# A 3x3 convolution with 2x2 max pooling: a new instruction order, casts moved from VectorE to ScalarE, and a wait added on GpSimd

## The chip, the cores and the metric

The kernel runs on one core of a Trainium2 chip. The metric is the device time of one execution in microseconds (us); lower is better. The kernel before takes 102.99 us (median of 3 runs, 102.98 to 103.02).

The core has five instruction streams that run at the same time, each strictly in its own program order: TensorE (PE in the profile: matmuls, with PEld for its weight loads), VectorE (DVE), ScalarE (ACT), GpSimd (POOL) and SyncE (SP, which here only issues DMAs). They meet through semaphores.

## The reference

```python
x_pad = np.pad(x, ((0, 0), (0, 0), (1, 1), (1, 1)))          # x: 16 x 64 x 64 x 64
for kh in range(3):
    for kw in range(3):
        conv[b, co] += weight[co, ci, kh, kw] * x_pad[b, ci, kh:kh+64, kw:kw+64]
output[b, c, i, j] = np.max(conv[b, c, 2*i:2*i+2, 2*j:2*j+2])  # 16 x 128 x 32 x 32
```

The input has 64 channels, the output 128. All is float32; the kernel multiplies in bf16.

## The kernel before, in words

**Tiles.** Two images lie in the 128 partitions (2 x 64 channels), so there are eight image pairs. A pair is cut into four stretches of eight output rows; the 32 stretches are numbered s = 0 to 31 (s // 4 is the pair, except that 2 and 3 stand for the last and the third stretch of pair 0). Each stretch has two halves h = 0, 1, one per image: a matmul uses 64 rows of the array, and two such matmuls, one per half, run beside each other. A step is named with its stretch and half: `P2.7.1` is product P2 of stretch 7, image 1.

**The computation of a stretch.** An even and an odd conv row of a pooled pair share input rows, and max(a, b) is formed from sums and differences of rows. For most stretches ("W" in `TYPES`) three row tensors are made first: a sum (`S.s`, tile ws), a difference (`E.s`, tile we) and the differences of rows two apart (`D.s`, tile wd, twice as large). Each can be made on VectorE (line 88) or on GpSimd (line 89); three tuples of stretch numbers choose. Stretches of type "K" need only a sum on VectorE (`KS.s`, tile ks) and read the rows themselves. The weights are combined to match: `g0`, `g1`, `g2` are the three kernel rows cast to bf16, `D2`, `D0`, `GM`, `GP` their sums and differences; PE transposes each block (`T...`, line 165) and ScalarE or VectorE copies it from PSUM to the tile wt (`V...`, lines 182 to 188).

**The chain of a half stretch.** PE accumulates the first products into a PSUM bank (P2 and P0, or PA1 and PA2). ScalarE copies that bank, after P2, into a second bank (`SE`, line 389) and, after P0, into SBUF with a sign (`EV`, lines 373 and 375), which frees the first bank. PE adds P3 to the second bank; VectorE takes the row maximum of bank and SBUF copy (`MX`, line 399); PE adds P1 (or PR), the product of the row sum. ScalarE copies the odd columns out (`OD`, line 405), VectorE takes the column maximum (`CM`, line 419), which frees the second bank, and SyncE stores the stretch (`ST`). There are eight banks.

**The first image pair** goes another way, in pieces: its rows come as float32 in three tiles, kfirst (two loads), ksecond (two) and middle (three). The K stretches 0 and 2 need bf16 rows, so kfirst and ksecond are cast into the tile kx0: `XOa`, `XOb`, `XEa`, `XEb` (odd and even rows of kfirst, first and second part) and `X1a`, `X1b`, `X2a`, `X2b` for ksecond. Their products are done in half stretches, `F.k.part` for stretch 0, `H.k.part` for stretch 2, six matmuls each. Stretch 1 lies in middle: `Ea`, `Eb`, `Da`, `Db`, `S.1` make its row tensors, `G.k.part` are its products, `SEa`, `SEb` its copies. PR.0 and PR.2 finish stretches 0 and 2.

**The order.** Nothing is scheduled by a compiler: the text `ORDER` lists every step, and each engine runs its steps in that order. Tile adds waits only where data or buffers ask for them, plus one kind that is written by hand: every row operation that the kernel routes through `on_gpsimd` waits for the last operation routed through `on_vector`, so that a GpSimd row operation starts only when VectorE's last one is done.

**Loads.** `LX.p.part` (line 124) loads half an image pair, converting to bf16, from GpSimd's queue; the seven first loads and all stores are issued by SyncE. `L` is the third load of middle; it waits for the cast `XOa`. `LX.1.0` waits for the cast `XOb`.

Of the kernel before, what the change touches and what calls it, by code (L numbers as in the profile page):

```python
# [11 lines left out]
def kernel(  # L12
# [11 lines left out]
    nc = tc.nc  # L24
# [47 lines left out]
    odd_cast = {}  # L72
# [69 lines left out]
    def slots(m):  # L142
        return wq[:, m : m + 3, :]
# [302 lines left out]
            queue.dma_start(out=dst[:, h : h + 1], in_=src[:, h : h + 1])  # L446


    def cast_rows(n, src, to, lo, hi):
        out, in_ = kx0[:, to + lo : to + hi : 2, :], src[:, lo:hi:2, :]  # L450
        if n in CAST_BY_SCALAR:
            odd_cast[n] = nc.scalar.copy(out=out, in_=in_)
        else:
            odd_cast[n] = nc.vector.tensor_copy(out=out, in_=in_)  # L454

    steps = {
        "g0": lambda: nc.scalar.copy(out=slots(G0), in_=g0),
        "g1": lambda: nc.vector.tensor_copy(out=slots(G1), in_=g1),  # L458
        "g2": lambda: nc.scalar.copy(out=slots(G2), in_=g2),
        "D2": lambda: sbuf_sum(True, out=slots(D2), in0=g2, in1=g1, op=SUB),  # L460
        "D0": lambda: sbuf_sum(True, out=slots(D0), in0=g0, in1=g1, op=SUB),
        "GS": lambda: sbuf_sum(False, out=gsum, in0=g0, in1=g2, op=ADD),
# [28 lines left out]
    for m in PRODUCTS:  # L491
        steps[m] = lambda s, h, m=m: product(m, s, h)

    ORDER = """
        D0 g2 g0 TD0 g1 D2 TD2 VD0 XEa uG1 TG1 F.2.0 TG0 XOa L VD2 F.0.0 TG2 GS GP uGP VG1 XOb F.0.1 LX.1.0 VG2
        VG0 F.1.0 F.1.1 XEb F.2.1 EV.0.1 EV.0.0 GM uGM LX.2.0 F.3.1 F.3.0 TMP VMP KS.0 X1a X2a X1b X2b KS.2
        H.0.0 H.1.0 H.0.1 H.1.1 EV.2.1 EV.2.0 Ea LX.1.1 LX.3.0 Da MX.0.0 MX.0.1 H.2.0 PR.0.1 H.3.0 G.0.0 Eb
        G.0.1 H.2.1 H.3.1 PR.0.0 SEa.0 SEa.1 SEb.0 SEb.1 E.3 P2.3.1 G.1.0 S.1 MX.2.0 OD.0.0 CM.0.0 G.2.0 OD.0.1
        CM.0.1 ST.0 LX.3.1 LX.2.1 Db G.1.1 EV.1.1 MX.2.1 G.2.1 MX.1.1 PR.2.0 PA1.4.0 PA2.4.0 EV.1.0 MX.1.0
        PA1.4.1 P1.1.0 PR.2.1 OD.2.0 CM.2.0 SE.3.1 P1.1.1 EV.4.0 S.3 OD.2.1 CM.2.1 ST.2 OD.1.0 CM.1.0 OD.1.1  # L500
        CM.1.1 ST.1 D.3 P0.3.1 PB1.4.0 EV.3.1 P2.3.0 P3.3.1 MX.3.1 PA2.4.1 SE.3.0 PB2.4.0 MX.4.0 EV.4.1 E.5
        P2.5.1 P2.5.0 SE.5.0 P1.3.1 PB1.4.1 P0.3.0 EV.3.0 D.5 P0.5.0 SE.5.1 EV.5.0 E.8 OD.3.1 PB2.4.1 KS.4
        PR.4.0 OD.4.0 P3.5.0 P0.5.1 EV.5.1 D.7 P3.5.1 E.7 P2.7.1 P2.7.0 D.8 D.9 SE.7.0 CM.3.1 CM.4.0 MX.4.1
        PR.4.1 MX.5.0 P3.3.0 MX.3.0 SE.7.1 P0.7.1 MX.5.1 P0.7.0 EV.7.0 P3.7.1 P3.7.0 P1.3.0 MX.7.0 OD.4.1 CM.4.1
        EV.7.1 MX.7.1 S.5 P1.5.1 P1.5.0 OD.5.1 CM.5.1 OD.3.0 CM.3.0 OD.5.0 CM.5.0 ST.5 ST.4 S.7 P1.7.0 E.6
        P2.6.0 P2.6.1 OD.7.0 CM.7.0 D.6 LX.7.1 LX.4.0 LX.6.0 LX.4.1 S.6 D.10 D.11 S.11 E.9 KS.12 PA1.12.1 P1.7.1
        PA1.12.0 PA2.12.1 SE.6.1 P3.6.1 P0.6.1 SE.6.0 OD.7.1 PA2.12.0 EV.12.0 EV.12.1 CM.7.1 P2.8.0 SE.8.0
        P0.6.0 EV.6.0 P3.6.0 P0.8.0 PB1.12.1 PB2.12.1 P2.8.1 P3.8.0 MX.6.0 P1.6.0 EV.6.1 P2.9.1 PB1.12.0 MX.6.1
        P1.6.1 MX.12.1 PR.12.1 EV.8.0 MX.8.0 PB2.12.0 SE.8.1 P0.8.1 OD.6.0 CM.6.0 OD.6.1 CM.6.1 MX.12.0 SE.9.1
        P0.9.1 OD.12.1 CM.12.1 S.8 E.10 P1.8.0 OD.8.0 CM.8.0 S.14 S.10 D.14 P3.8.1 P3.9.1 P2.10.0 EV.8.1 SE.10.0  # L510
        EV.9.1 PR.12.0 OD.12.0 MX.8.1 P1.8.1 P2.9.0 SE.9.0 P0.10.0 EV.10.0 P2.10.1 LX.5.0 MX.9.1 S.9 E.14 E.11
# [81 lines left out]
```

## Time and profile before

| | |
|---|---|
| median of 3 runs | 102.99 us (102.98 to 103.02) |
| the profiled execution | 103.01 us |
| its span, first to last instruction | 101.1 us |
| TensorE clock granted, mean | 0.993 of full |
| PE, DVE, ACT, POOL busy | 93%, 89%, 86%, 69% of the span |
| HBM read, written | 17.20 MB, 8.39 MB |

The profile is one execution. "start us, us" in a timeline row are the start from the span's begin and the length of a run of like instructions (x6: six of them); in brackets stands how long the engine had been idle and what ended that. In a row of groups come busy time, mean length in ns, idle time before. L207 is line 207 of the kernel; in the changed kernel lines from 449 on stand up to six lower.

### The profile page before, as it was taken

The numbers are of one execution on the slowest core, as the hardware profiler recorded it, in microseconds if no ns is written. First come the engines' busy times: TensorE is split into PE (matmuls) and PEld (weight loads), VectorE is DVE, ScalarE is ACT, GpSimd is POOL, SyncE is SP. The second block draws the span as 40 slices with busy tenths as digits, with TensorE's granted clock in tenths as the row PEclk, the third lists the DMA queues.
The fourth block names the chain that finished last, engine by engine and source line by source line (L and its number), as shares of the span: only waits on it lengthen the run. The fifth ranks groups of instructions, "written<-read, shape, count | busy, mean of one in ns | idle before, by whom it ended". The sixth has DMA issues, their size and how long they took to land.

```text
span 101.1 us, 2529 instructions
## 1 busy us (share of the span) xinstructions
PE 94.3 (93%) x903; PEld 58.9 (58%) x903; DVE 89.9 (89%) x190; ACT 86.0 (85%) x194; POOL 70.2 (69%) x79
## 2 busy tenths in 40 slices
PE   6889999999999999999999999999999999999900
PEld 2257878844555656777678677675555546545500
DVE  1589989999999999999999989999898969999950
ACT  5356778999699899999999999898999999999830
POOL 7268999906995985774987693994969699417000
PEclk9999999999999999999999999999999999999997
DMA  2999899999947999999947984835024837423062
GB/s 58 297 342 300 171 199 216 221 232 226 244 78 131 247 228 220 228 221 358 343 31 124 282 180 42 169 114 208 3 76 141 304 111 252 163 104 110 0 227 84
DMA packets 11900, 18.41 MB, mean 182 GB/s; under 512 B 880, under 2 KB 9200, under 8 KB 11888
## 3 DMA queue, kind: packets, MB, share of 16 engines
q0 software_dynamic: 2016, 7.34, 39.9%
q1 hardware_dynamic: 9728, 10.78, 32.0%
q8 instruction: 7, 0.11, 0.4%
q10 hardware_dynamic: 144, 0.13, 0.4%
q14 instruction: 5, 0.04, 0.1%
HBM read 17.20 MB, written 8.39 MB: 253 GB/s over the span
## 4 chain that ended last, share of the span: by engine, by line
PE 87%; DVE 4%; DMA 3%; ACT 1%; issue 1%; DVEq 0%; ACTq 0%
PE acc L207 86%; DMA wraw<-in_weight_dram 3%; DVE acc L399 1%; PE acc L165 1%; DVE wq L88 1%; DVE o L434 1%; DVE kx L454 1%; ACT acc L389 1%; ACT od L427 1%; DVE wq L458 0%; DVE wt L188 0%; DVEq L399 0%; ACTq L389 0%
## 5 line engine op out<-in xcount | busy, mean ns | idle before, releaser
L207 PEld LDWEIGHTS <-wt 64*128 64x128 bf16 x870 | 56.4, 94 | 32.6 <-issue 4.7
L207 PE MATMUL acc<-wd,wt 64*128 64x512 bf16 (+2 forms) x336 | 65.9, 369 | 0.1
L399 DVE TENSOR_TENSOR acc<-acc,ev 128x512 f32<-128x512 f32 x64 | 42.4, 692 | 1.4 <-ACT ev L375 0.5
L207 PE MATMUL acc<-we,wt 64*128 64x512 bf16 (+3 forms) x168 | 39.2, 369 | 0.0
L207 PE MATMUL acc<-ws,wt 64*128 64x512 bf16 (+3 forms) x168 | 37.7, 369 | 0.2 <-DVE acc L399 0.2
L375 ACT ACTIVATE ev<-acc 128x512 f32<-128x512 f32 x54 | 32.2, 607 | 1.4 <-PE acc L207 1.2
L389 ACT COPY acc<-acc 128x512 f32<-128x512 f32 x52 | 30.7, 596 | 0.9 <-DVE o L419 0.2
L419 DVE TENSOR_TENSOR o<-acc,od 128x256 f32<-128x256 f32 x62 | 24.4, 417 | 2.4 <-ACT od L405 1.5
L89 POOL TENSOR_TENSOR ws<-xb 128x512 bf16<-128x512 bf16 x15 | 17.1, 1148 | 11.6 <-DVE wd L88 7.3
L405 ACT COPY od<-acc 128x256 f32<-128x256 f32 x62 | 22.5, 382 | 2.1 <-PE acc L207 1.8
L89 POOL TENSOR_TENSOR we<-xb 128x512 bf16<-128x512 bf16 x16 | 18.4, 1150 | 6.0 <-PE acc L207 2.3
L89 POOL TENSOR_TENSOR wd<-xb 128x1024 bf16<-128x1024 bf16 x9 | 19.1, 2123 | 1.9 <-DVE we L88 1.1
L207 PE MATMUL acc<-xb,wt 64*128 64x504 bf16 (+3 forms) x72 | 15.0, 372 | 0.0
L88 DVE TENSOR_TENSOR wd<-xb 128x1024 bf16<-128x1024 bf16 x16 | 10.7, 682 | 0.0
L124 POOL DMA_DIRECT2D xb<-in_x_dram x14 | 7.9, 574 | 0.1
L207 PE MATMUL acc<-ks,wt 64*128 64x504 bf16 (+1 forms) x30 | 7.2, 377 | 0.0
L373 ACT COPY ev<-acc 128x512 f32<-128x512 f32 x10 | 5.6, 590 | 1.4 <-PE acc L207 1.3
L207 PE MATMUL acc<-kx,wt 64*128 64x252 bf16 (+3 forms) x96 | 6.0, 267 | 0.4 <-DVE kx L454 0.4
L89 POOL TENSOR_TENSOR wd<-middle 128x512 bf16<-128x512 f32 (+1 forms) x3 | 4.9, 1643 | 0.2 <-DVE we L88 0.2
L551 PE MATMUL acc<-const-bfloat16-1.0 128*128 128x512 bf16 x8 | 3.5, 621 | 0.8 <-PEq L574 0.8
L88 DVE TENSOR_TENSOR ws<-xb 128x512 bf16<-128x512 bf16 x10 | 4.1, 418 | 0.0
L88 DVE TENSOR_TENSOR we<-xb 128x512 bf16<-128x512 bf16 x9 | 3.7, 425 | 0.0
(33 smaller groups left out, 29.4 us busy)
## 6 DMA issues: line engine op xcount, KB each, us to landing
out_dram<-o SPq DMA_DIRECT2D x31, 256.0 KB, 2.9
xb<-in_x_dram POOLq DMA_DIRECT2D x7, 528.0 KB, 9.0
xb<-in_x_dram POOLq DMA_DIRECT2D x7, 496.0 KB, 11.0
middle<-in_x_dram SPq DMA_DIRECT2D x1, 512.0 KB, 5.3
ksecond<-in_x_dram SPq DMA_DIRECT2D x1, 320.0 KB, 5.8
middle<-in_x_dram SPq DMA_DIRECT2D x1, 320.0 KB, 6.2
wraw<-in_weight_dram SPq DMA_DIRECT2D x1, 288.0 KB, 2.9
kfirst<-in_x_dram SPq DMA_DIRECT2D x1, 288.0 KB, 3.2
```

The lines of the kernel that those rows point to most:

```text
L88: return on_vector(nc.vector.tensor_tensor(**args))
L89: return on_gpsimd(nc.gpsimd.tensor_tensor(**args))
L124: inst = nc.gpsimd.dma_start(out=xb[p][:, 1 + lo : 1 + hi, :], in_=rows_of(p, lo, hi))
L165: nc.tensor.transpose(tp[:, k * CO : (k + 1) * CO], wq[:, j : j + 2, :].rearrange("a b c -> a (b c)"), ident,)
L207: nc.tensor.matmul(acc[t][:, i0:i1, o0:o1], wt[lo : lo + CI, tap_of(m0, kw, h), :], rows(lo, i0, i1, c0, c1), start=start and kw == 1, sto ...
L373: nc.scalar.copy(out=ev[s, h], in_=acc[t])
L375: nc.scalar.mul(ev[s, h], acc[t], -1.0)
L389: nc.scalar.copy(out=acc[tb[s, h]], in_=acc[ta[s, h]])
L399: nc.vector.tensor_tensor(out=t, in0=t, in1=ev[s, h], op=MAX)
L405: nc.scalar.copy(out=od[s, h], in_=acc[tb[s, h]][:, :, 1::2])
L419: nc.vector.tensor_tensor(out=ot[s][:, h], in0=acc[t][:, :, 0::2], in1=od[s, h], op=MAX)
L551: nc.tensor.matmul(acc[n].rearrange("p a b -> p (a b)"), ones[:, 0:128], ones, start=True, stop=True, skip_group_check=True)
```

## The change

Four things change; the arithmetic and the number of matmuls (903) do not.

1. `ORDER` is replaced by another list of the same steps, with other banks and other loads as a consequence. GpSimd's loads are issued as 1.0, 1.1, 2.0, 5.1, 2.1, 3.0, 3.1, 4.0, 5.0, 4.1, 6.0, 7.0, 6.1, 7.1 instead of 1.0, 2.0, 1.1, 3.0, 3.1, 2.1, 7.1, 4.0, 6.0, 4.1, 5.0, 5.1, 6.1, 7.0. The first store stands after stretch 6 instead of after stretch 0.
2. The tuples of row work: GpSimd makes 15 sums as before, 17 differences (16 before) and 9 whole wd tensors (10 before); VectorE one wd more and one difference fewer.
3. The casts: XEa, XEb, X1a, X1b, X2a, X2b go from VectorE to ScalarE, XOb from ScalarE to VectorE; g1 stays on VectorE and g0, g2 on ScalarE. The four weight blocks copied out by ScalarE are the same.
4. The casts of weights and rows that stay on VectorE now pass through `on_vector`, so that GpSimd's next row operation waits for them.

```diff
-    SUM_ON_GPSIMD = (5, 7, 8, 9, 10, 14, 15, 18, 19, 20, 23, 24, 28, 29, 30,)
-    DIFF_ON_GPSIMD = (5, 6, 8, 10, 15, 16, 17, 18, 19, 20, 22, 25, 27, 28, 29, 30,)
-    EDGES_ON_VECTOR = (7, 8, 9, 10, 11, 14, 15, 17, 18, 19, 23, 24, 27, 29, 30, 31,)
-    TURNED_BY_SCALAR = ("D2", "G1", "G2", "MP")
-    CAST_BY_SCALAR = ("XOb",)
+    SUM_ON_GPSIMD = (5, 6, 7, 8, 10, 16, 17, 19, 22, 23, 24, 25, 27, 28, 31,)
+    DIFF_ON_GPSIMD = (5, 7, 8, 10, 11, 13, 15, 17, 18, 19, 22, 23, 24, 25, 26, 29, 30,)
+    EDGES_ON_VECTOR = (5, 6, 7, 8, 9, 10, 13, 15, 17, 18, 19, 23, 25, 26, 27, 30, 31,)
+    TURNED_BY_SCALAR = ("D2", "G2", "MP", "G1")
+    CAST_BY_SCALAR = ("g0", "g2", "XEa", "XEb", "X1a", "X1b", "X2a", "X2b")
...
+    def tap_cast(n, m, src):
+        if n in CAST_BY_SCALAR:
+            nc.scalar.copy(out=slots(m), in_=src)
+        else:
+            on_vector(nc.vector.tensor_copy(out=slots(m), in_=src))
...
-            odd_cast[n] = nc.vector.tensor_copy(out=out, in_=in_)
+            odd_cast[n] = on_vector(nc.vector.tensor_copy(out=out, in_=in_))
...
-        D0 g2 g0 TD0 g1 D2 TD2 VD0 XEa uG1 TG1 F.2.0 TG0 XOa L VD2 F.0.0 TG2 GS GP uGP VG1 XOb F.0.1 LX.1.0 VG2
+        D2 TD2 g0 TG0 D0 TD0 g2 TG2 XOa L VD2 F.0.0 VG0 F.1.0 XEa VD0 F.2.0 GS XOb F.1.1 LX.1.0 F.0.1 LX.1.1 GM
```

**VectorE, the first instructions.** In the rows kx is the tile of cast rows (kx0), wq the bf16 weights before the transposition, wt after it, acc a PSUM bank. Before, from the first weight sum to the difference Ea of middle:

```order
L88 TENSOR_TENSOR wq<-wraw 128x192
L458 CAST wq<-wraw 128x192
L88 TENSOR_TENSOR wq<-wraw 128x192
L188 COPY wt<-acc_84 128x512
L454 CAST kx_132<-kfirst 128x5x64
L454 CAST kx_132<-kfirst 128x4x64
L88 TENSOR_TENSOR wq<-gsum,wraw 128x192
L188 COPY wt<-acc_88 128x512
L454 CAST kx_132<-kfirst 128x4x64
L88 TENSOR_TENSOR wq<-gsum,wraw 128x192
L88 TENSOR_TENSOR ks<-kx_132 128x512
L454 CAST kx_132<-ksecond 128x5x64 x2
```

And of the change, from GM to the row maxima of stretch 2, the twelve rows in front of PR.2:

```order
L88 TENSOR_TENSOR wq<-gsum,wraw 128x192
L88 TENSOR_TENSOR ks<-kx_132 128x512
L88 TENSOR_TENSOR wq<-gsum,wraw 128x192
L453 CAST wq<-wraw 128x192
L399 TENSOR_TENSOR acc_85<-acc_85,ev 128x512
L399 TENSOR_TENSOR acc_86<-acc_86,ev 128x512
L88 TENSOR_TENSOR we<-middle 128x256
L88 TENSOR_TENSOR ks<-kx_132 128x512
L88 TENSOR_TENSOR we<-middle 128x256
L325 TENSOR_REDUCE ws<-middle 128x512
L88 TENSOR_TENSOR we<-middle 128x512
L399 TENSOR_TENSOR acc_88<-acc_88,ev 128x512
```

The casts of ksecond are gone from this engine, and the second half of the difference (Eb, the second `we<-middle 128x256`), the sum S.1 and the difference E.3 now stand between the row maxima of stretch 0 (acc_85, acc_86) and those of stretch 2 (acc_88, then acc_84).

**ScalarE, the first instructions of the change**, behind the casts g0 and g2:

```order
L184 COPY wt<-acc_84 128x512
L458 CAST kx_132<-kfirst 128x5x64
L458 CAST kx_132<-kfirst 128x4x64
L184 COPY wt<-acc_87 128x512
L373 COPY ev<-acc_84 128x512
L373 COPY ev<-acc_88 128x512
L458 CAST kx_132<-ksecond 128x5x64
L458 CAST kx_132<-ksecond 128x4x64
L458 CAST kx_132<-ksecond 128x5x64
L458 CAST kx_132<-ksecond 128x3x64
L182 ACTIVATE wt<-acc_91 128x2x384
L184 COPY wt<-acc_87 128x384
```

Six casts stand among the copies; before there was one (XOb), behind the copies of D2 and G1.

**GpSimd, from the sum gsum to the first row operation.** xb_110 is the tile of pair 1, xb_111 of pair 2, and so on. Before:

```order
L149 COPY wq<-wq 128x64
L89 TENSOR_TENSOR gsum<-wraw 128x192
L149 COPY wq<-wq 128x64
L124 DMA xb_110<-in_x_dram 128x2112
L149 COPY wq<-wq 128x64
L124 DMA xb_111<-in_x_dram 128x2112
L124 DMA xb_110<-in_x_dram 128x1984
L124 DMA xb_112<-in_x_dram 128x2112
L89 TENSOR_TENSOR wd<-middle 128x512
```

Of the change:

```order
L89 TENSOR_TENSOR gsum<-wraw 128x192
L124 DMA xb_110<-in_x_dram 128x2112
L124 DMA xb_110<-in_x_dram 128x1984
L149 COPY wq<-wq 128x64 x3
L124 DMA xb_111<-in_x_dram 128x2112
L124 DMA xb_114<-in_x_dram 128x1984
L124 DMA xb_111<-in_x_dram 128x1984
L89 TENSOR_TENSOR wd<-middle 128x512 x2
```

Both loads of pair 1 now stand directly behind gsum, ahead of all three weight copies (L149).

More of the change, by code (lines that the diff above doesn't have):

```diff
@@ L453, in cast_rows @@
         else:
-            odd_cast[n] = nc.vector.tensor_copy(out=out, in_=in_)
+            odd_cast[n] = on_vector(nc.vector.tensor_copy(out=out, in_=in_))
     steps = {
-        "g0": lambda: nc.scalar.copy(out=slots(G0), in_=g0),
-        "g1": lambda: nc.vector.tensor_copy(out=slots(G1), in_=g1),
-        "g2": lambda: nc.scalar.copy(out=slots(G2), in_=g2),
+        "g0": lambda: tap_cast("g0", G0, g0),
+        "g1": lambda: tap_cast("g1", G1, g1),
+        "g2": lambda: tap_cast("g2", G2, g2),
         "D2": lambda: sbuf_sum(True, out=slots(D2), in0=g2, in1=g1, op=SUB),
@@ L494 @@
     ORDER = """
-        D0 g2 g0 TD0 g1 D2 TD2 VD0 XEa uG1 TG1 F.2.0 TG0 XOa L VD2 F.0.0 TG2 GS GP uGP VG1 XOb F.0.1 LX.1.0 VG2
[L496 to L499, printed above, removed]
@@ L545 @@
-        P1.29.1 OD.30.0 CM.30.0 EV.31.1 MX.31.1 EV.31.0 MX.31.0 Q.0 Q.1 OD.30.1 CM.30.1 ST.30 OD.29.0 CM.29.0
-        OD.29.1 CM.29.1 ST.29 ODh.0.0 CMh.0.0 ODh.0.1 CMh.0.1 ODh.1.0 CMh.1.0 ODh.1.1 ST.31.0 CMh.1.1 ST.31.1
+        D2 TD2 g0 TG0 D0 TD0 g2 TG2 XOa L VD2 F.0.0 VG0 F.1.0 XEa VD0 F.2.0 GS XOb F.1.1 LX.1.0 F.0.1 LX.1.1 GM
+        uGM XEb KS.0 GP g1 VG2 F.3.1 EV.0.0 F.2.1 F.3.0 MX.0.0 EV.0.1 MX.0.1 Ea uG1 TG1 X1a H.0.0 H.1.0 uGP TMP
+        LX.2.0 LX.5.1 X1b H.1.1 X2a X2b KS.2 H.2.0 H.2.1 VMP VG1 PR.0.1 H.0.1 EV.2.0 EV.2.1 H.3.0 G.0.0 SEa.1
@@ new lines @@
+        SEa.0 H.3.1 PR.0.0 OD.0.0 OD.0.1 Eb S.1 LX.2.1 G.0.1 Da G.1.0 SEb.1 SEb.0 E.3 MX.2.1 MX.2.0 CM.0.0
+        CM.0.1 S.3 PR.2.1 PR.2.0 OD.2.0 CM.2.0 OD.2.1 CM.2.1 Db G.2.1 P2.3.0 G.1.1 G.2.0 PA1.4.1 EV.1.1 MX.1.1
+        PA1.4.0 PA2.4.1 EV.1.0 MX.1.0 D.3 E.5 LX.3.0 LX.3.1 KS.4 D.7 E.6 D.6 PA2.4.0 PB1.4.1 P2.3.1 SE.3.0
+        EV.4.0 P0.3.0 P3.3.0 PB1.4.0 PB2.4.0 PB2.4.1 EV.4.1 MX.4.1 P1.1.1 SE.3.1 P0.3.1 P1.1.0 LX.4.0 EV.3.0
+        P3.3.1 MX.3.0 P1.3.0 MX.4.0 PR.4.0 E.7 P2.7.1 PR.4.1 OD.1.1 CM.1.1 EV.3.1 MX.3.1 P1.3.1 OD.1.0 CM.1.0
@@ L547 @@
+        MX.29.1 P3.30.0 P3.30.1 EV.30.1 MX.30.1 SE.31.0 P0.31.0 P2.31.1 P3.31.0 EV.30.0 S.30 MX.30.0 SE.31.1
+        P1.29.1 OD.29.1 CM.29.1 P0.31.1 P3.31.1 P1.29.0 P1.30.1 P1.30.0 EV.31.0 MX.31.0 EV.31.1 MX.31.1 S.31 Q.0
+        Q.1 ST.20 ST.27 ST.19 ST.22 ST.28 OD.29.0 CM.29.0 ST.29 OD.30.1 CM.30.1 OD.30.0 CM.30.0 ST.30 ODh.0.0
+        CMh.0.0 ODh.0.1 CMh.0.1 ODh.1.0 CMh.1.0 ODh.1.1 ST.31.0 CMh.1.1 ST.31.1
     """
```

85 lines of the change are left out of this document (40 added, 45 removed).

## The prediction

> **What bounds the kernel now.** I read the page first, then the chain that ended last, then the stages.
>
> ```profile
> span 101.1 us, 2529 instructions
> PE 94.3 (93%) x903; PEld 58.9 (58%) x903; DVE 89.9 (89%) x190; ACT 86.0 (85%) x194; POOL 70.2 (69%) x79
> DMA  2999899999947999999947984835024837423062
> PE 87%; DVE 4%; DMA 3%; ACT 1%; issue 1%; DVEq 0%; ACTq 0%
> ```
>
> PE bounds the span, with VectorE and ScalarE close behind; DMA is full for the first eleven slices (28 us). The chain in order of time shows what lies around the matmuls:
>
> ```profile
> 0.74 2.88 DMA wraw<-in_weight_dram
> ...
> 5.29 0.78 DVE kx L454
> ...
> 6.11 0.51 PE acc L207 x6
> ...
> 95.41 0.86 PE acc L207 x12
> ```
>
> A start of 6.11 us in which the weights land and are cast, transposed and copied; then matmuls to 96.3; then a tail of pooling and the last store. Busy PE is not PE at its peak, so I count matmuls per stage:
>
> ```profile
> 45.00:60.00 15.00, 15.00 (x141) 10.99 (x139) 14.33 (x29) 14.82 (x36) 11.30 (x11) 1.00 0.89 227
> ...
> 75.00:90.00 15.00, 14.99 (x134) 8.28 (x132) 13.34 (x28) 14.86 (x35) 10.91 (x8) 1.00 0.55 194
> ```
>
> (The columns are the stretch, its length, then busy time and instructions of PE, PEld, DVE, ACT, POOL.) 141 matmuls in 15 us are 0.106 us each. In 75 to 90 there are 134: 7 x 0.106 = 0.74 us of hidden stalls. So the middle has at most about 0.7 us to give, and everything to lose; a gain must come mainly from the start. "At" a time is from the span's start; the execution itself took 103.01 us for its span of 101.1, 0.02 over the median of the runs, so a shift of the span goes straight onto 103.01.
>
> **The start of PE.** Before, PE waits for the cast XEa. The first four rows are of kfirst (length min/median/max in ns, then first and last start) and of its loads' times to landing:
>
> ```profile
> L454 DVE CAST kx<-kfirst x3: 271/285/848, 5.2 to 7.3; 128x256 bf16<-128x256 f32 x2, 128x320 bf16<-128x320 f32 x1
> L100 SPq DMA_DIRECT2D kfirst<-in_x_dram x1: 423/423/423, 1.6 to 1.6; - x1
> L452 ACT CAST kx<-kfirst x1: 419/419/419, 6.3 to 6.3; 128x256 bf16<-128x256 f32 x1
> ...
> DMA to landing us min/median/max: 3.2/3.7/4.2
> ```
>
> And from the timeline:
>
> ```profile
> 5.04 0.80 POOL L89 TENSOR_TENSOR gsum<-wraw 128x192 f32<-128x192 f32 x1
> 4.29 0.38 PE L165 MATMUL acc<-ident,wq 128*128 128x128 bf16 x4
> 7.75 0.58 ACT L184 COPY wt<-acc 128x512 bf16<-128x512 bf16 x1 [1.03 <-PE acc L165]
> ```
>
> XEa took 0.848 us where its neighbours took 0.271 and 0.285: it started at 5.21, while gsum ran on GpSimd from 5.04 to 5.84, and ended just after it. In the change gsum waits for XOa, so nothing casts beside it, and the first product needs D2, transposed first: PE starts the four transposes at 4.29 as before, they end at 4.67, ScalarE's copy starts 0.04 later and takes 0.58, and F.0.0 can start at about 5.34, as XOa ends near 4.75 (kfirst's first part, issued half a us before the second, lands in 3.2, near 4.4). That is **0.77 us earlier** than 6.11. The other transposes lie ahead of it instead of between products.
>
> **From there to the first image's end.** ScalarE now casts: 0.419 us where VectorE took 0.271 to 0.285 for 256 columns. The six new casts less XOb are 5 x 0.42 = 2.1 us more for it; they lie where it waited (1.03 us ahead of the copy at 7.75 alone). VectorE loses the casts of ksecond and two of kfirst, gains XOb, one wd and loses one we:
>
> ```profile
> L454 DVE CAST kx<-ksecond 128x320 bf16<-128x320 f32 (+2 forms) x4 | 1.0, 318 | 0.0
> L88 DVE TENSOR_TENSOR wd<-xb 128x1024 bf16<-128x1024 bf16 x16 | 10.7, 682 | 0.0
> L88 DVE TENSOR_TENSOR we<-xb 128x512 bf16<-128x512 bf16 x9 | 3.7, 425 | 0.0
> L89 POOL TENSOR_TENSOR wd<-xb 128x1024 bf16<-128x1024 bf16 x9 | 19.1, 2123 | 1.9 <-DVE we L88 1.1 <-PE acc L207 0.7
> L89 POOL TENSOR_TENSOR we<-xb 128x512 bf16<-128x512 bf16 x16 | 18.4, 1150 | 6.0 <-PE acc L207 2.3 <-DVE wd L88 1.5 <-issue 1.4
> ```
>
> VectorE: 1.0 + 0.85 + 0.28 - 0.28 - 0.68 + 0.43 = 1.6 us less. GpSimd: 2.12 - 1.15 = 0.97 us less. None of this is on the path by itself; it is cover for the stalls of the middle.
>
> What is late next? The waits on VectorE between Eb and PR.2, shown in the order above: PR.2 needs both row maxima of stretch 2, and ahead of them stand Eb, S.1 and E.3. Eb needs the second load of middle:
>
> ```profile
> 9.69 0.42 DVE L88 TENSOR_TENSOR we<-middle 128x256 bf16<-128x256 f32 x1
> 10.02 1.29 DVE L399 TENSOR_TENSOR acc<-acc,ev 128x512 f32<-128x512 f32 x2
> 11.22 1.13 DVE L88 TENSOR_TENSOR we<-middle 128x256 bf16<-128x256 f32 x2
> 12.27 1.24 DVE L325 TENSOR_REDUCE ws<-middle 128x512 bf16<-128x1024 f32 x1
> 3.54 0.43 SPq L109 DMA_DIRECT2D middle<-in_x_dram  x1
> middle<-in_x_dram SPq DMA_DIRECT2D x1, 256.0 KB, 6.4
> ```
>
> That load was issued at 3.54 and landed 6.4 later, at 9.94. VectorE gets to Eb at about 10.0 (ScalarE casts X2b by 9.8, KS.2 follows), so with the same landing Eb starts at 9.98. Eb and E.3 together take 12.27 - 11.22 = 1.05, S.1 1.16 to the next start, the two maxima 1.29: 3.50, and 0.05 to PE. PR.2 starts at 9.98 + 3.55 = 13.53. PE itself is ready a little earlier. Its halves take 0.33 us (36 matmuls in about 2.0, last row below), so F.0 and F.1 end near 7.1; X1a stands behind the two copies EV.0 (1.07 for such a pair) and ends at about 8.6, where H.0.0 starts. Eleven halves (3.6), six transposes (0.5; four took 0.38) and PR.0 (6 x 0.106 = 0.64) bring PE to 13.4. After PR.2 (0.64) and three halves (0.99) comes the first product of pair 1, at 15.16. The same amount of work came before at 16.07, the first row here:
>
> ```profile
> 16.07 1.00 PE L207 MATMUL acc<-xb,wt 64*128 64x512 bf16 x7
> 8.76 1.07 ACT L373 COPY ev<-acc 128x512 f32<-128x512 f32 x2 [0.43 <-PE acc L207]
> 7.64 2.06 PE L207 MATMUL acc<-kx,wt 64*128 64x256 bf16 x36
> ```
>
> So the lead is **0.91 us** if the load lands at 9.94, and it shrinks one for one with a later landing: none is left from 10.85 on.
>
> **Will it land at 9.94?** LX.1.0 was issued at 7.03; now it waits only for XOb (kfirst's second part lands at 1.6 + 4.2 = 5.8, the cast takes 0.28), so it starts near 6.2, and LX.1.1 right behind it.
>
> ```profile
> 7.03 0.70 POOL L124 DMA_DIRECT2D xb<-in_x_dram  x1
> 8.00:9.00 1.00, 1.00 (x26) 0.92 (x22) 1.00 (x5) 0.57 (x2) 0.91 (x3) 1.00 1.28 381
> 9.00:10.00 1.00, 1.00 (x20) 0.72 (x14) 0.97 (x4) 0.83 (x2) 1.00 (x2) 1.00 0.98 184
> q0 software_dynamic: 2, 0.01, 146.6%
> q1 hardware_dynamic: 8, 0.02, 51.4%
> ```
>
> DMA is full at 8 to 9 us (share 1.28). The last two rows are the queues of the stretch 9.5 to 9.6: GpSimd's queue has 2 packets of 10 there, 2.5 us after its issue; with the issue 0.85 earlier it bites from about 8.2, while the middle load still has 1.74 us to go. Bounds: nothing taken, 9.94; half of the turns taken, 8.2 + 2 x 1.74 = 11.7. I take the fifth of packets that the row shows: 8.2 + 1.74 / 0.8 = 10.4, nearer to the first. Then the lead at pair 1 is 0.91 - 0.46 = 0.45 us.
>
> [...]
>
> **The middle and the tail.** The new waits on GpSimd for VectorE's casts cost only at gsum (behind it on GpSimd stand LX.1.0 and LX.1.1): it starts after XOa, at 4.8, and before at 5.04, so nothing is lost. From pair 1 on both kernels run the same products; I cost the rest at nothing net, between +0.74 (the stalls of 75 to 90 gone) and the third rival. The tail ends in the same steps: two row maxima, the 12 matmuls of Q, the halves of OD and CM, one store.
>
> **Forecast: 103.01 - 0.45 = 102.56, say 102.6 us**; with the two bounds of the landing 102.1 and 103.9.
>
> **Rivals.**
> 1. *More than the lead.* The 1.6 us taken off VectorE also clears the stalls of 75 to 90: 103.01 - 0.91 - 0.74 = 101.4 at best. For it: VectorE is busy 14.33 of 15 us from 45 to 60; against: in 75 to 90 it is busy 13.34 only, so its load is not what stalls there.
> 2. *GpSimd's loads overtake middle* (slower). With LX.1.0 and LX.1.1 in the engines from 8.2 and half of the turns, Eb starts at 11.7, PR.2 at 15.3, pair 1 at 16.9: 0.85 late, 103.9. It decides from a landing of 10.85. For it: DMA share 1.28 before the overlap; against: 2 of 10 packets.
> 3. *Lead given back (no change).* In the change the edge difference D.10 on VectorE reads LX.2.1, the fifth load, and the row maximum of stretch 7 stands behind it. The fifth load before:
>
> ```profile
> 11.41 1.12 POOL L124 DMA_DIRECT2D xb<-in_x_dram  x2
> xb<-in_x_dram POOLq DMA_DIRECT2D x1, 496.0 KB, 14.3
> 15.33 4.85 SPq L443 DMA_DIRECT2D out_dram<-o  x3
> ...
> L419 DVE TENSOR_TENSOR o<-acc,od 128x256 f32<-128x256 f32 x62 | 24.4, 417 | 2.4 <-ACT od L405 1.5
> ```
>
>    It landed at 11.41 + 14.3 = 25.7. VectorE reaches D.10 at about 15.6 + eleven pairs of products at 0.65 (6 x 0.106), the last of them with P1.3.1, then 0.4 each for OD and CM (the row of CM says 0.417) and 0.68 each for D.5 and D.9, or 24.9. If the landing stays, VectorE waits 0.8 and behind it P1.7 and S.8, with perhaps 0.4 of slack: 0.4 lost, 103.0. Against: the three stores that shared these 10 us (the row of L443) now come later, so the load should be about 1 us earlier.
>
> That the change would not do what it says can be excluded for the cast: gsum stands behind XOa by a wait.
>
> **How the numbers follow.** Forecast (a lead of 0.2 to 0.9): 0.45. Rival 1 (over 0.9): 0.11. No change, from rival 3 or a landing near 10.85: 0.16. Rival 2 with anything of that sign in the middle: 0.28. About 0.2% (0.2 us) can be told from no change here. So faster 0.56, same 0.16, slower 0.28. The range reaches from rival 1's best, 101.4, to a little over rival 2, 104.0.
>
> **What would show it.** Right: XOa near 0.27 us and F.0.0 at about 5.3; the second middle load at 10.2 to 10.6; the first product of xb at about 15.6; D.10 without a wait; 141 matmuls in most stretches of 15 us. Wrong: the middle load past 10.9, VectorE idle ahead of Eb or D.10, or fewer matmuls per 15 us after 30 us, where I expect none.

## The result, and the profile after

The changed kernel took 102.33 us (median of 13 executions, 102.03 to 102.92) beside 103.02 of before on the same chip: a ratio of 0.9942, 95% interval 0.9921 to 0.9963. A second set, further down as "again", gave 102.63 beside 103.12, ratio 0.9946 (0.9914 to 0.9977). So it is faster by 0.5 to 0.7 us, where 0.45 had been forecast (102.6). The size came out, in part by luck; the way to it did not, and the spread is the first sign of that: the middle half of the 25 executions of the changed kernel lies between 102.25 and 102.83, that of the 36 of before in those two sets between 102.97 and 103.19.

The profiled execution of the changed kernel is one of the long ones, 102.92 us for a span of 101.1. The head of its page:

```profile
span 101.1 us, 2518 instructions
...
PE 94.8 (94%) x903; PEld 58.1 (57%) x903; DVE 88.9 (88%) x185; ACT 86.8 (86%) x199; POOL 68.7 (68%) x79
...
DMA  2999999999999999998999933805000344079062
...
PE 88%; ACT 5%; DVE 2%; issue 1%; ACTq 0%
```

As before, PE bounds; VectorE is 1.0 us lighter, ScalarE 0.8 heavier, GpSimd 1.5 lighter. Chain and busy times alone look like before, so I read the start row by row. PE first (start, length, engine, line, operation, number merged into the row, the wait ahead of it):

```profile
0.78 3.57 PE L557 MATMUL acc<-const-bfloat16-1.0 128*128 128x512 bf16 x8 [0.78 <-PEq L580]
4.30 1.86 PE L165 MATMUL acc<-ident,wq 128*128 128x128 bf16 x16
6.09 2.90 PE L207 MATMUL acc<-kx,wt 64*128 64x256 bf16 x48
...
9.53 0.83 PE L207 MATMUL acc<-kx,wt 64*128 64x256 bf16 x12 [0.26 <-ACT kx L458]
...
13.93 0.51 PE L207 MATMUL acc<-we,wt 64*128 64x256 bf16 x6 [0.15 <-ACT acc L395]
...
14.71 0.82 PE L207 MATMUL acc<-ks,wt 64*128 64x512 bf16 x6
```

```profile
16.54 0.38 PE L207 MATMUL acc<-xb,wt 64*128 64x512 bf16 x1
```

The first transposes start at 4.30, as forecast. But 16 take 1.86 us, 0.105 from start to start; in before four took 0.38, 0.055 from start to start. They run at half rate, like the warm-up matmuls ahead of them (0.43 us from start to start for 512 columns, 0.21 in the products of xb), and the first product F.0.0 comes at 6.09 instead of 5.34, the first product of xb at 16.54 instead of 15.6: 0.47 later than the 16.07 of before. What then stood between the two, on ScalarE and on VectorE:

```profile
8.05 1.07 ACT L373 COPY ev<-acc 128x512 f32<-128x512 f32 x2 [1.26 <-PE acc L207]
9.01 1.39 ACT L458 CAST kx<-ksecond 128x320 bf16<-128x320 f32 x4
...
12.26 1.07 ACT L373 COPY ev<-acc 128x512 f32<-128x512 f32 x2 [0.24 <-PE acc L207]
```

```profile
9.10 1.30 DVE L399 TENSOR_TENSOR acc<-acc,ev 128x512 f32<-128x512 f32 x2 [1.14 <-PE acc L207]
...
10.98 0.42 DVE L88 TENSOR_TENSOR we<-middle 128x256 bf16<-128x256 f32 x1
11.31 1.23 DVE L325 TENSOR_REDUCE ws<-middle 128x512 bf16<-128x1024 f32 x1
12.46 0.83 DVE L88 TENSOR_TENSOR we<-middle 128x512 bf16<-128x512 f32 x1
13.36 1.30 DVE L399 TENSOR_TENSOR acc<-acc,ev 128x512 f32<-128x512 f32 x2
```

X1a is the first of the four casts at 9.01, behind both copies EV.0; it ends at 9.48 and H.0.0 starts at 9.53 on it. Eb starts at 10.98, and from 9.10 on VectorE has no gap until PR.2. The cast, gsum and the loads:

```profile
L460 DVE CAST kx<-kfirst x2: 282/288/294, 4.9 to 6.1; 128x256 bf16<-128x256 f32 x2
```

```profile
5.27 0.81 POOL L89 TENSOR_TENSOR gsum<-wraw 128x192 f32<-128x192 f32 x1 [2.51 <-DVE kx L460]
```

```profile
middle<-in_x_dram SPq DMA_DIRECT2D x1, 256.0 KB, 6.3
```

XOa is short (0.29) and gsum starts behind it: that step holds. The second load of middle took 6.3 us where it took 6.4 before, and landed at 9.88 (9.91 before), not at 10.4. And the end:

```profile
75.00:90.00 15.00, 15.00 (x140) 9.13 (x135) 13.82 (x31) 14.83 (x37) 10.29 (x8) 1.00 0.26 89
```

```profile
95.50 0.81 PE L207 MATMUL acc<-ws,wt 64*128 64x256 bf16 x11 [0.21 <-DVE acc L399]
```

140 matmuls in 75 to 90 us where before had 134. From the first product of xb to this last product pass 95.50 - 16.54 = 78.96 us; in before 95.41 - 16.07 = 79.34. So in this execution the start lost 0.47 and the rest, which I had costed at nothing, won 0.38 of it back.

### The profile page after: what moved, and what is told of

Read it like the earlier page. It is cut to its first block, busy times and chain, and to the rows that moved or that the text cites. A ratio compares the mean times of both kernels' runs of the same rounds, so it can differ in the third digit from the quotient of the medians.

```text
span 101.1 us, 2518 instructions
## 1 busy us (share of the span) xinstructions
PE 94.8 (94%) x903; PEld 58.1 (57%) x903; DVE 88.9 (88%) x185; ACT 86.8 (86%) x199; POOL 68.7 (68%) x79
## 4 chain that ended last, share of the span: by engine, by line
PE 88%; ACT 5%; DVE 2%; issue 1%; ACTq 0%
PE acc L207 82%; PE acc L557 4%; PE acc L165 2%; ACT ev L373 2%; DVE acc L399 1%; ACT acc L389 1%; DVE o L434 1%; ACT od L427 1%; ACT acc L395 1%; ACT ev L375 1%; ACT od L405 0%; ACT kx L458 0%; ACTq L389 0%
## 5 line engine op out<-in xcount | busy, mean ns | idle before, releaser
L207 PEld LDWEIGHTS <-wt 64*128 64x128 bf16 x870 | 54.9, 94 | 34.3 <-issue 4.7
L207 PE MATMUL acc<-we,wt 64*128 64x512 bf16 (+3 forms) x168 | 40.5, 369 | 0.2 <-ACT acc L395 0.2
L207 PE MATMUL acc<-ws,wt 64*128 64x512 bf16 (+3 forms) x168 | 38.3, 369 | 0.2 <-DVE acc L399 0.2
L375 ACT ACTIVATE ev<-acc 128x512 f32<-128x512 f32 x54 | 32.8, 617 | 0.9 <-PE acc L207 0.6
L389 ACT COPY acc<-acc 128x512 f32<-128x512 f32 x52 | 31.6, 609 | 1.8 <-DVE o L419 1.0
L89 POOL TENSOR_TENSOR we<-xb 128x512 bf16<-128x512 bf16 x17 | 19.4, 1149 | 6.6 <-DVE we L88 2.9
L89 POOL TENSOR_TENSOR wd<-xb 128x1024 bf16<-128x1024 bf16 x8 | 17.0, 2123 | 2.9 <-DVE wd L88 2.9
L207 PE MATMUL acc<-xb,wt 64*128 64x504 bf16 (+3 forms) x72 | 12.5, 372 | 0.0
L88 DVE TENSOR_TENSOR wd<-xb 128x1024 bf16<-128x1024 bf16 x17 | 11.4, 682 | 0.0
L207 PE MATMUL acc<-ks,wt 64*128 64x504 bf16 (+1 forms) x30 | 5.7, 376 | 0.0
```

Source lines behind the costliest of these rows:

```text
L88: return on_vector(nc.vector.tensor_tensor(**args))
L89: return on_gpsimd(nc.gpsimd.tensor_tensor(**args))
L207: nc.tensor.matmul(acc[t][:, i0:i1, o0:o1], wt[lo : lo + CI, tap_of(m0, kw, h), :], rows(lo, i0, i1, c0, c1), start=start and kw == 1, sto ...
L375: nc.scalar.mul(ev[s, h], acc[t], -1.0)
L389: nc.scalar.copy(out=acc[tb[s, h]], in_=acc[ta[s, h]])
```

## The experiments

Three theories were left. **The start**: the gain is made ahead of pair 1. **The rest**: it is made by order and split behind it. **The grant**: the moment at which PE gets its full clock differs from one execution to the next (6.51 us in the changed kernel's profile, 4.10 in before's) and decides what the start is worth. Ratios are to before in the same set, with 95% intervals.

### again: the changed kernel once more

No edit.

> The changed kernel once more. Theory of the grant: PE begins each execution at half clock, and the moment at which the full clock is granted differs from execution to execution; in the one that was profiled it came at about 6.5 us (16 transposes 0.105 us apart), in before's at about 4.1. Then the times spread from about 102.0 to 102.9 again, in the order of that moment, while before's spread within 0.4; a profile with a grant before 4.5 us shows the 16 transposes in about 1.0 us and the first product at about 5.3. Rival (the order itself makes the transposes slow): they take 1.8 us in every profile, whatever the time. Both: median 102.2 to 102.5.

102.63 us (102.00 to 103.45), ratio 0.9946 (0.9914 to 0.9977). The profiled execution was the longest, 103.45, and told two more things. PE, then VectorE:

```profile
4.34 1.21 PE L166 MATMUL acc<-ident,wq 128*128 128x128 bf16 x16
6.03 2.87 PE L208 MATMUL acc<-kx,wt 64*128 64x256 bf16 x48 [0.48 <-DVE kx L461]
```

```profile
26.65 0.69 DVE L89 TENSOR_TENSOR wd<-xb 128x1024 bf16<-128x1024 bf16 x1 [0.80 <-DMA xb<-in_x_dram]
```

(Lines are one higher here.) The 16 transposes took 1.21 us, so the order itself doesn't make them slow. The clock record of the trace begins with the grant of the full clock, which is why the profile's clock column reads 1.00 ahead of it: 4.69 us here, 6.51 in the profile above, 4.10 in before. But kfirst's first part landed at 5.66 instead of 4.87, so the first product waited for XOa instead. And D.10 waited 0.80 us for LX.2.1, which landed at 26.63 instead of 23.72: the third rival, with the wait that it had named, in one of the two profiles. From P3.6 to P1.5 PE took 4.34 us there and 3.64 in the profile above, so it cost 0.7, where 0.4 had been put on it. So the grant isn't the only thing that spreads the times.

The executions that weren't profiled can be asked too, since the span L and the mean granted clock c of each are on record. With 1.00 up to the fall to half clock and 0.5 behind it (at 98.67 us in the changed kernel's profile, which reads 1.00 ahead of that and 0.50 from 99 on), the fall lies at L x (2c - 1), and the grant 92.16 or 95.57 us ahead of that (the two lengths that the traces show, last section). For the execution above that is 101.1 x 0.976 = 98.7, less 92.16 = 6.5, as in its trace. In the profiles of kernels with the warm-up the grant lies between 3.85 and 6.71, which mostly leaves one of the two lengths. The first set, with the grants so worked out to about 0.1 us:

| grant | time |
|---|---|
| 4.2, 4.4, 5.0 | 102.28, 102.23, 102.22 |
| 4.9 or later (clock 1.000), twice | 102.32, 102.33 |
| 5.6, 5.8, 6.0 | 102.61, 102.59, 102.60 |
| 6.2, 6.2, 6.5 | 102.79, 102.85, 102.92 |
| 3.5 or 6.9; 3.6 or 7.0 | 102.16; 102.03 |

In the first set the time goes with the grant. In both sets together, eight executions with a grant of 3.9 to 5.0 have a median of 102.33 and seven with 5.8 to 6.5 one of 102.81; four of the eight, all of them in the second set, took 102.38 to 103.45, the last being the one profiled here, so an early grant isn't enough. The kernel before hardly follows: 27 of its executions beside the experiments with a grant of 3.8 to 5.0 have a median of 103.03, 17 with 5.8 to 6.5 one of 103.11. What the change wins is thus about 0.7 us with an early grant and 0.3 with a late one.

### head_only and rest_only: the order cut at MX.1.0

```
head_only: ORDER = after's up to MX.1.0, then before's without those steps; split of before
rest_only: ORDER = before's up to MX.1.0, then after's without those steps; split of after
```

> The start of the changed kernel, up to the last row maximum of stretch 1 (with its casts, turns and waits), then the rest in the order and split of before. Theory of the start (the prediction's): the gain is made before pair 1, so 102.4, all of the 0.6. Theory of the rest: the start's lead is lost by 28 us and the gain comes from the order and split of the middle and tail: 103.0. Both halves: 102.7.

> The start of before, up to the last row maximum of stretch 1, then the rest in the order and split of the changed kernel. Theory of the start: 103.0. Theory of the rest: 102.4. If the two parts add up, this and the kernel with the start alone lie together 0.6 under twice the time of before.

104.89 (ratio 1.016, 1.011 to 1.021) and 106.11 (1.027, 1.022 to 1.032): both slower than either kernel, so the two totals divide nothing. The joint costs more than the difference sought: in rest_only VectorE's first edge differences wait for loads that the other start had issued earlier.

```profile
DVE wd L88 <- DMA xb<-in_x_dram: 1.6, 2, 1.0
```

The splice of head_only also changes part of what is accumulated behind the joint (which part was not traced), so it computes something else than the reference. Up to the joint, though, its steps are those of the changed kernel one for one, and its profile caught an early grant, at 3.85 us:

```profile
4.36 1.05 PE L165 MATMUL acc<-ident,wq 128*128 128x128 bf16 x16 [0.19 <-DVE wq L88]
5.42 2.85 PE L207 MATMUL acc<-kx,wt 64*128 64x256 bf16 x48
```

```profile
15.80 0.38 PE L207 MATMUL acc<-xb,wt 64*128 64x512 bf16 x1
```

This is the start that I had forecast: the first product at 5.42 (5.34), X1a's end at 8.74 (8.6), Eb at 10.24, the first product of xb at 15.80 (15.6), a lead of 0.27.

### no_cast_wait: without the wait of GpSimd for VectorE's casts

```diff
-            on_vector(nc.vector.tensor_copy(out=slots(m), in_=src))
+            nc.vector.tensor_copy(out=slots(m), in_=src)
-            odd_cast[n] = on_vector(nc.vector.tensor_copy(out=out, in_=in_))
+            odd_cast[n] = nc.vector.tensor_copy(out=out, in_=in_)
```

> The changed kernel without the wait of GpSimd's next instruction for VectorE's casts: gsum goes as soon as the weights are there and D0 is done, at about 4.3 instead of 5.27, and runs beside XOa. Theory of the start: XOa takes about 0.8 us again instead of 0.29 and ends at about 5.4; with an early grant the first product comes 0.2 to 0.4 later, 102.6. Rival (the wait is worth nothing, the order already keeps them apart): 102.3.

102.74 (102.29 to 104.58), ratio 0.9965 (0.9938 to 0.9992), beside 0.9946 with the wait: the intervals overlap, so no cost of taking it away is shown. The collision did not come in the profile:

```profile
L460 DVE CAST kx<-kfirst x2: 277/280/283, 4.5 to 6.2; 128x256 bf16<-128x256 f32 x2
```

```profile
4.69 0.81 POOL L89 TENSOR_TENSOR gsum<-wraw 128x192 f32<-128x192 f32 x1 [1.92 <-DVE wq L88]
```

XOa started at 4.53, ahead of gsum, and kept its 0.28. By these rows, and by XEa in before, which started 0.17 into gsum and took 0.85, it would be longer only where kfirst lands while gsum runs (an estimate).

### before_wait: the wait alone, in the kernel before

```diff
-        "g1": lambda: nc.vector.tensor_copy(out=slots(G1), in_=g1),
+        "g1": lambda: on_vector(nc.vector.tensor_copy(out=slots(G1), in_=g1)),
-            odd_cast[n] = nc.vector.tensor_copy(out=out, in_=in_)
+            odd_cast[n] = on_vector(nc.vector.tensor_copy(out=out, in_=in_))
```

> The kernel before with one part of the change alone: GpSimd's next instruction with two SBUF inputs waits for VectorE's last cast, so gsum waits for XOa. Theory of the start (the prediction's first step): XEa takes 0.28 us instead of 0.85, the first product starts at about 5.5 instead of 6.11, and 0.2 to 0.5 of it reaches the end: 102.5 to 102.8. Rival (what follows gsum is 0.8 later and the chains of ScalarE and VectorE behind the first image set PR.2 anyway): 102.9 to 103.2, no change.

102.87 beside 103.07, ratio 0.9964 (0.9931 to 0.9997): about 0.2 to 0.4 us faster, at the edge of what can be told. The casts of kfirst, PE's first product and its first product of xb:

```profile
L454 DVE CAST kx<-kfirst x3: 279/283/347, 5.3 to 7.5; 128x256 bf16<-128x256 f32 x2, 128x320 bf16<-128x320 f32 x1
```

```profile
5.72 0.50 PE L207 MATMUL acc<-kx,wt 64*128 64x256 bf16 x6
```

```profile
16.04 1.01 PE L207 MATMUL acc<-xb,wt 64*128 64x512 bf16 x7
```

XEa takes 0.35 instead of 0.85 (not 0.28: it casts 320 columns, its neighbours 256) and the first product comes at 5.72, 0.39 earlier, although the weights' own chain was 0.12 later here (first transposes at 4.41). The first step of the prediction holds. In this execution the lead was gone at 16.04 (16.07 before): LX.1.0 landed at 15.99, 1.1 later than in before's profile, and PE's weight load waited 0.5 for it.

### no_warm: without the warm-up matmuls

```diff
-    for n in range(8):
+    for n in range(0):
```

> The changed kernel without its 8 warm-up matmuls, whose product nobody uses. Theory of the grant: PE's work begins at 4.3 us instead of 0.8, so the full clock comes about 3.5 us later, at 7 to 10.5 instead of 3.6 to 7; the transposes and the first image's products run at half rate until then: 0.8 to 1.6 us more than the median of the changed kernel, 103.2 to 104.2, and the transposes 0.105 us apart in the profile. Rival (the clock of the first 7 us is hidden by the loads and casts): 102.5.

104.01 (103.85 to 104.26), ratio 1.010 (1.009 to 1.011), 1.4 to 1.7 us over the changed kernel. The grant came at 8.28 us:

```profile
4.31 1.87 PE L165 MATMUL acc<-ident,wq 128*128 128x128 bf16 x16 [4.31 <-DVE wq L88]
6.11 3.76 PE L207 MATMUL acc<-kx,wt 64*128 64x256 bf16 x48
```

```profile
17.41 0.38 PE L207 MATMUL acc<-xb,wt 64*128 64x512 bf16 x1
```

```profile
96.36 0.81 PE L207 MATMUL acc<-ws,wt 64*128 64x256 bf16 x11 [0.21 <-DVE acc L399]
```

The 48 matmuls of the first image take 3.76 us instead of 2.90, and all of it arrives at pair 1: (17.41 - 16.54) / (8.28 - 6.51) = 0.49 us for each us by which the grant is later. The rest takes 96.36 - 17.41 = 78.95 again. The clock of the first 7 us isn't hidden in this kernel.

### splits_back: before's split in the changed order

```diff
-    SUM_ON_GPSIMD = (5, 6, 7, 8, 10, 16, 17, 19, 22, 23, 24, 25, 27, 28, 31,)
+    SUM_ON_GPSIMD = (5, 7, 8, 9, 10, 14, 15, 18, 19, 20, 23, 24, 28, 29, 30,)
...
```

> The changed kernel with the three tables of before: which of the sums, differences and edge differences of stretches 5 to 31 run on GpSimd and which on VectorE. The order, the casts and the waits stay changed. Theory that the split makes the gain of the last 20 us (before lost 1.24 us between the products of stretch 24 and the last one, the changed kernel 0.82): VectorE has 1.6 us more, some of it ahead of waiting products, 103.0 or more. Theory of the start: the split is worth nothing, 102.4.

127.49 us (124.19 to 128.93), beside 102.99. Each engine runs its steps in the order of the text, and a step that changes its engine stands among other steps there: GpSimd now waits for VectorE's differences (14.1 us in two waits) and PE for GpSimd's edge differences (7.7 in three).

```profile
POOL ws L89 <- DVE we L88: 14.1, 2, 11.0
...
PE acc L207 <- POOL wd L89: 7.7, 3, 3.6
```

Neither theory had this. It shows that before's split doesn't fit the changed order, not what the changed split is worth, and where the 0.38 us of the rest come from can't be put down to the one or the other by it.

### s1_late and start2: S.1 out of VectorE's chain, X1a and X1b off ScalarE

```
s1_late: ... MX.2.1 MX.2.0 CM.0.0 CM.0.1 S.1 S.3 ...          (S.1 stood behind Eb)
start2:  the same, and ... F.3.0 X1a X1b MX.0.0 ...           (both behind TG1 before, on ScalarE; now VectorE)
```

> The changed kernel with the row sum S.1 (1.23 us on VectorE) behind the two row maxima of stretch 2 and the column maxima of stretch 0 instead of ahead of them. Theory of VectorE's chain (the prediction's: Eb, S.1, E.3 and the maxima bound the products PR.2): PR.2 starts 0.8 to 1.2 us earlier, 101.6 to 101.9. Rival (ScalarE's chain: casts, then the copies EV.2, of which the second ends 0.04 after E.3): the maxima wait for EV.2.1 instead, nothing is gained, 102.4.

> As s1_late, and the casts X1a and X1b run on VectorE, ahead of the first row maximum, where VectorE waited 1.14 us, instead of on ScalarE behind both copies EV.0. Theory of ScalarE's chain: H.0.0 starts 0.6 us earlier, right behind TG1, and EV.2, the seeds SEa and SEb and PR.2 with it: 101.8. Theory of VectorE's chain: as s1_late. If a lead at pair 1 is eaten later by the loads or by the engines' load: 102.4.

103.86 (ratio 1.008, 1.005 to 1.011) and 103.67 (1.006, 1.004 to 1.009): slower, which neither theory had. In s1_late VectorE, then PE:

```profile
13.35 1.30 DVE L399 TENSOR_TENSOR acc<-acc,ev 128x512 f32<-128x512 f32 x2 [1.22 <-ACT ev L373]
...
15.22 2.38 DVE L325 TENSOR_REDUCE ws<-middle 128x512 bf16<-128x1024 f32 x2
17.51 0.74 DVE L419 TENSOR_TENSOR o<-acc,od 128x256 f32<-128x256 f32 x2
```

```profile
17.98 0.59 PE L207 MATMUL acc<-xb,wt 64*128 64x512 bf16 x4 [0.64 <-DVE o L419]
```

The maxima of stretch 2 start at 13.35, as in the changed kernel (13.36): with S.1 gone VectorE waits 1.22 for the copy EV.2.1. So both chains end there together, as the rival had it. And S.1 beside S.3 delays the column maxima of stretch 2, whose banks PA1.4 needs: 0.8 us lost at 17 us. S.1 stood in a gap that cost nothing.

### x1_vector, lx51_late, both

```
x1_vector: X1a, X1b on VectorE ahead of MX.0.0; S.1 in its place
lx51_late: LX.5.1 ahead of LX.5.0 instead of behind LX.2.0
both:      the two together
```

> The changed kernel with the casts X1a and X1b on VectorE, ahead of the first row maximum, and nothing else changed (S.1 in its place). Theory of ScalarE's chain: the row maxima of stretch 2 waited 1.33 us for the copy EV.2.1 in the kernel start2, which is the room that S.1 (1.23 us) and E.3 had, so with S.1 in its place VectorE is no later and H.0.0, EV.2, the seeds and PR.2 all come about 0.5 us earlier: 0.5 under the changed kernel beside the same runs of before, ratio 0.990. Theory of VectorE's chain: the chain from the first row maximum to PR.2 has no gap, the two casts (0.55 us) push it or nothing is won: ratio 0.994 to 0.998.

> The changed kernel with the load LX.5.1 (used from stretch 22 on, at about 60 us) issued ahead of LX.5.0 instead of as the fourth, so that LX.2.1 and the three loads behind it land about 2.4 us earlier. Theory that D.10's wait for LX.2.1 makes the long executions (it waited 0.80 in the one of 103.45, nothing in the one of 102.92): no execution over 103.1, median 0.1 to 0.3 lower, 102.2 to 102.4. Rival (the grant alone makes the spread): the same median and spread as the changed kernel, 102.0 to 103.4.

> The edits of x1_vector and lx51_late together. If both theories hold and add: 101.7 to 101.9, ratio 0.987 to 0.989, faster than both kernels of the study. If the lead is eaten behind pair 1: ratio 0.994.

x1_vector 102.39 (102.31 to 102.55), ratio 0.9942 (0.9930 to 0.9954); lx51_late 102.68 (102.38 to 104.18), 0.9969 (0.9944 to 0.9993); both 102.63 (102.02 to 103.17), 0.9961 (0.9937 to 0.9984). None can be told from the changed kernel by its median; LX.2.1 earlier leaves long executions, so D.10's wait doesn't make all of them. The profile of lx51_late, whose start is the changed kernel's, has a grant in the middle, at 5.31:

```profile
4.36 1.49 PE L165 MATMUL acc<-ident,wq 128*128 128x128 bf16 x16
5.79 2.72 PE L207 MATMUL acc<-kx,wt 64*128 64x256 bf16 x48
```

```profile
16.05 0.38 PE L207 MATMUL acc<-xb,wt 64*128 64x512 bf16 x1
```

```profile
95.00 0.81 PE L207 MATMUL acc<-ws,wt 64*128 64x256 bf16 x11 [0.21 <-DVE acc L399]
```

Again 95.00 - 16.05 = 78.95 for the rest. In x1_vector H.0.0 follows the transposes without a wait:

```profile
8.87 0.83 PE L207 MATMUL acc<-kx,wt 64*128 64x256 bf16 x12
```

```profile
15.88 0.38 PE L207 MATMUL acc<-xb,wt 64*128 64x512 bf16 x1
```

H.0.0 comes 2.93 us behind the first product (5.94), in lx51_late 3.25; pair 1 comes 9.94 behind it, in lx51_late 10.26. That is 0.32 us won ahead of pair 1. The profile of both, 102.02 us with the grant at 4.80, shows it again (15.57 - 5.64 = 9.93):

```profile
4.41 1.22 PE L165 MATMUL acc<-ident,wq 128*128 128x128 bf16 x16
5.64 2.72 PE L207 MATMUL acc<-kx,wt 64*128 64x256 bf16 x48
```

```profile
15.57 0.38 PE L207 MATMUL acc<-xb,wt 64*128 64x512 bf16 x1
```

```profile
94.62 0.81 PE L207 MATMUL acc<-ws,wt 64*128 64x256 bf16 x11 [0.21 <-DVE acc L399]
```

The rest takes 0.1 longer in these two (94.62 - 15.57 = 79.05). At the same grant, worked out as above, about 0.2 us is left in the times of this set: with 5.5 and 6.1 lx51_late took 102.48 and 102.77, x1_vector 102.31 and 102.55. These are few executions, lx51_late and both have longer ones beside them (103.05 and more) at a grant of about 5, and the medians hide the difference behind such spread.

## Why the prediction was right, and where it was not

Profiles of the changed kernel's start, by the grant (times in us; the landing is that of kfirst's first part):

| profile | grant | 16 transposes | landing | first product | first product of xb |
|---|---|---|---|---|---|
| forecast | not considered | 0.9 (16 x 0.055) | 4.4 | 5.34 | 15.6 |
| head_only | 3.85 | 1.05 | 5.02 | 5.42 | 15.80 |
| again | 4.69 | 1.21 | 5.66 | 6.03 | 16.42 |
| lx51_late | 5.31 | 1.49 | 4.41 | 5.79 | 16.05 |
| after | 6.51 | 1.86 | 4.87 | 6.09 | 16.54 |
| no_warm | 8.28 | 1.87 | 4.67 | 6.11 | 17.41 |

1. **The start of PE.** The collision is real: without it XEa takes 0.35 instead of 0.85 (before_wait). The step that failed is "the first product needs D2, transposed first: PE starts the four transposes at 4.29 as before, they end at 4.67". It took the rate of one execution in which the full clock came at 4.10. The change puts all 16 transposes together right behind the warm-up, where a late grant nearly doubles them (1.86 instead of 1.05); in before only 4 stood there, and the others fell between waits. Nor was the landing of kfirst fixed: 4.37 to 5.66 in the profiles.
2. **The lead at pair 1.** Forecast 0.45; measured 0.27 with an early grant, 0.02 with one in the middle, -0.47 with a late one, and -0.35 in again, where kfirst landed late. The chain that I named (Eb, S.1, E.3, the maxima) does end at PR.2, but ScalarE's chain through EV.2.1 ends with it, and taking S.1 out gained nothing. "VectorE gets to Eb at about 10.0" was 0.2 (head_only) to 1.0 us early. And from Eb to the first product of xb the sum had 15.16 - 9.98 = 5.18; head_only, lx51_late and after show 5.56, 5.48 and 5.56, x1_vector, whose ScalarE is earlier, 5.24. The term that it lacked is ScalarE's chain: EV.2.1 ahead of the maxima, and the seed SEb, for which the weights behind PR.2 wait 0.50 (0.34 in x1_vector).
3. **The landing of middle.** The second load landed at 9.88 in the changed kernel's profile, not 10.4. GpSimd's first packet moved at 9.3, not 8.2: LX.1.0 was issued at 6.71, not 6.2, and its first packet came 2.6 behind the issue, where before's came 1.9 behind. Eb was late because VectorE's maxima were, so a wrong cause stood for a delay of about the right size (Eb forecast at 10.44, found at 10.24 to 10.98). Rival 2 falls with this landing. The two queues hardly met: of the 61 packets that moved from 9.3 to this landing 7 were GpSimd's. So no run shows the half of the turns behind the late bound (11.7), which was an estimate of mine; 7 of 61 is less than the fifth that I took, too. The landing isn't fixed, though: in other profiles of this start it came at 9.18 to 10.95. Eb waited for it in none, but in no_cast_wait, which had the latest, E.3 waited 0.51 for the third load of middle (13.15 instead of 11.15).
4. **"I cost the rest at nothing net"** failed by 0.38 us: 78.95 to 78.96 from the first product of xb to the last product, in four profiles with starts 1.4 us apart (after, lx51_late, no_warm, no_cast_wait), where before took 79.34. It is of the kind of rival 1 (which had 0.74 for it). 140 matmuls instead of 134 in 75 to 90 us show part of the place; which edit makes it stays open, since split and order could not be taken apart. The sums of busy time were off as well, without being on the path: VectorE 1.0 us lighter instead of 1.6, ScalarE 0.8 heavier instead of 2.1, GpSimd 1.5 lighter instead of 0.97.
5. **Rival 3** is real (0.80 us of wait on D.10, as named; 0.7 lost on PE instead of 0.4), in one profile of two.

So about the forecast size came out, but with little of it from the start and 0.4 from the rest, not the other way round: two errors that cancel, which is luck. With the middle grant: 0.02 + 0.39 at the last product (95.41 - 95.00 = 0.41), and 102.44 us for that execution, 0.57 under before's. The other 0.16 lie behind the start of the last product's group: 7.60 us to the end of the execution in before's profile, 7.40 to 7.44 in four with the changed order; which step makes that was not traced. By the same terms the median execution, 102.33, would have its first product of xb at 102.33 - 7.42 - 78.95 = 15.96, a lead of 0.11 (an estimate).

What stays open: which edit makes the 0.4 of the rest. The shortest executions of the changed kernel (102.00 and 102.03) were not profiled, and their clocks allow a grant of 3.6 or of 7.0; that it was the early one is argued from the table, not shown. Nor was before profiled with a late grant; that it depends less on it is read from the clocks of its executions (103.03 and 103.11) and from its narrower spread.

## What to carry to other kernels

Ask of each work moved to the front of PE's queue at which clock it will run there, and take the rate of the worst execution, not of the one profile at hand. The mean clock that is on record with each execution's time told here, without a profile, at which moment the full clock came (5.2 us worked out for lx51_late, 5.31 in its trace). A lead in time has to be followed through every engine's chain to its end: two chains that end within 0.1 us of each other give nothing for the shortening of one. And an order, with the split that it was made for, is one thing: a piece of it put into another order cost 1.8 to 25 us here.

## What the runs showed of the hardware

The clock of PE: grant and return to half clock lie 92.160 us apart in the changed kernel's trace and 95.573 in before's. By one of these two lengths the mean clocks of head_only, again, lx51_late and no_warm give a grant at 3.76, 4.60, 5.22 and 8.31 us, where their traces have it at 3.85, 4.69, 5.31 and 8.28. In splits_back, whose clock read 0.956 in the mean and 0.89 from 30 to 45 us, the grant can't be worked out so. With the same warm-up from 0.78 on the grant came between 3.85 and 6.71 us, up to 2.9 us apart. The first product of xb came 0.41 us later for each us from lx51_late's grant to the changed kernel's ((16.54 - 16.05) / (6.51 - 5.31)), and 0.49 from there to no_warm's.

VectorE and GpSimd: XEa, which started while gsum ran, took 0.848 us (before), and 0.347 without it (before_wait). XOb took 0.282 behind gsum's end (the changed kernel's profile), but 0.468 where it started about half a us into gsum (again). XOa, which started 0.16 ahead of gsum, kept its 0.28 (no_cast_wait). gsum itself took 0.80 in before and 0.81 in the changed kernel and in no_cast_wait. So the casts that started while gsum ran were the longer ones in these profiles.
